# Eight samples' recurrence on the VectorE alone, and the convolution's layer norm freed of a wait for the merge

## The chip, the cores and the metric

The kernel is one program on one core of a Trainium2 chip. Its engines are TensorE (PE, matrix products), VectorE (DVE), ScalarE (ACT), GpSimd (POOL) and SyncE (SP, whose queue issues nearly all DMAs). Each engine takes its instructions in the order in which they stand in its queue and waits at an instruction until the semaphores of that instruction are reached. The metric is the time of one execution on the device in microseconds (us), as the median of several runs.

## The reference, cut to what matters

One layer of a hybrid decoder. 512 tokens of a prompt and one token each of 8 samples (520 columns in all) go through an RWKV-7 branch and a convolution branch side by side; both are projected, weighted by sigmoid gates (the merge) and sent through an output projection, a gate and a last norm. The two places that the change touches are the samples' recurrence step and the convolution's layer norm with its two SiLU gates:

```
def step(S, inp):                              # S: value_dim x key_dim, per sample and head
    r_t, w_t, k_t, v_t, a_t, b_t = inp
    sa = einsum('bhij,bhj->bhi', S, a_t)
    S = S * w_t[:, :, None, :] + sa[..., None] * b_t[:, :, None, :] + v_t[..., None] * k_t[:, :, None, :]
    return S, einsum('bhij,bhj->bhi', S, r_t)
...
cm = mean(cf); cv = mean(square(cf - cm))      # over the 1024 channels
cf = (cf - cm) * rsqrt(cv + LN_EPS) * cln_g + cln_b
cb = silu(cf) * silu(gate_b)
y_b = einsum('btc,cd->btd', cb, w_proj_b)
m = sigmoid(ga) * y_a + sigmoid(gb) * y_b      # ga, gb: the merge projections
h = x + einsum('btd,de->bte', m, w_out)
```

## The kernel before

Activations lie channels on partitions, 520 tokens along the free dimension. All large products run in a split form: each operand is a rounded high part and a low part (hi, lo for activations, wh, wl for weights), and each 128x128 weight block costs three pairs of matmuls of 260 columns, hi by wh, lo by wh, hi by wl (`step`, L211). For each weight tile ACT writes wh (L154) and DVE writes wl (a subtraction, recorded like all helper calls at L67). A `gemm` is 16 such steps (8 in the two projections of the branches), and its sum in PSUM (tile mm) is then taken by DVE.

The program runs in stages: a first accumulation; then for each of eight pairs of heads p the projections of that pair (`gemm`), beside which the prompt's recurrence of the pair (`wkv`) and the depthwise convolution (`conv`, 30 multiply-adds of DVE into tile c for each of 8 channel tiles) run as generators; then the rest of the 32 `merge` projections (DVE scales mm into p, ACT takes the sigmoid, SP stores it); then the projection of the RWKV branch (`gemm(8, ya)`), of the convolution branch (`gemm(8, yb)`), the output product, and the gate with the last norm.

The order of PE's and DVE's queues is written out by the program itself. `tick` is called once after each step and lets every live generator go on by one stretch: `yield n` means wait n steps, `yield ROOM` means go on in a later step, and only if the planned DVE clock is at most LAG = 1.0 us ahead of the planned PE clock. `Paced` charges both clocks; an operation that is issued through `gps` (GpSimd) is charged to the same DVE clock as one issued through `vec`. The weights' subtractions, the scaling of mm and the small operations of the prompt's recurrence are issued without asking for room. ACT, POOL and SP take their instructions in an order that the framework sets from the program.

The change lies in two generators. `sample` (two of them share the eight groups i0 of eight state rows) treats a group of 8 x 64 state entries per partition in nine operations of 128x512: t1 = s0\*a, t2 = v\*k, sa = sum(t1), s0 = s0\*w, t1 = sa\*b, t1 = t1 + t2, s0 = s0 + t1 (then stored by SP), t2 = s0\*r, oso = sum(t2). Four of the nine, t1 = s0\*a, t2 = v\*k, s0 = s0\*w and t2 = s0\*r, go through `gps`. `samples` starts the two, waits for both, and carries their output through PE and a small norm; `rest` runs `samples`, starts `reload` (the eight tiles ya for the first branch projection, each loaded, then split by ACT and DVE) and then runs `lnorm`. `rest` begins when the last pair's recurrence loop begins, with `conv` of the last channel tile not yet at its end.

`lnorm` sums tile csum over channels, subtracts the mean from the eight convolution tiles c, sums their squares, takes the reciprocal of the root (L865), waits until all merges are issued (`flag["merged"]`, L867), and then, for each tile, loads the gate gb (SP), scales c (DVE), applies gain and bias and the sigmoid (ACT), multiplies (DVE, then POOL with the gate), and splits the product into hi and lo (`hlp`) in the pool xp, whose buffers hold the layer's input until the last merge has read it.

The prompt's recurrence is what PE waits for step by step: for each of eight chunks, PE multiplies (aux<-suv,ar), ACT copies (xs, L642), five steps later PE multiplies (aux<-xs,ttb), ACT copies (suv, L648), five steps later PE multiplies (aux<-suv,bn), DVE writes the next suv, five steps later the next chunk begins (for the last pair; `ly`).

Of the kernel before, what the change touches and what calls it, by code (L numbers as in the profile page):

```python
# [12 lines left out]
ALU = mybir.AluOpType  # L13
# [4 lines left out]
P = 128  # L18
# [33 lines left out]
ROOM = -1  # L52
# [18 lines left out]
def body(nc, tc, a):  # L71
    with ExitStack() as es:
# [4 lines left out]
        xp = pool("xp", bufs=2 * KD)  # L77
# [19 lines left out]
        def work(us):  # L97
            clock["dve"] = max(clock["dve"], clock["pe"]) + us
# [4 lines left out]
        vec = Paced(nc.vector, lambda name, n: work(0.0069 * n if name == "reciprocal" else (0.2 if name == "scalar_tensor_tensor" else 0.14) + 0.00107 * n))  # L103
        gps = Paced(nc.gpsimd, lambda name, n: work(0.0014 * n if n > 64 else 0.05))
        pe = Paced(nc.tensor, pe_work)

        def tt(eng, out, x, y, op):
            eng.tensor_tensor(out, x, y, op=op)
# [189 lines left out]
        def colsum(lhsT, hi, lo, n):  # L298

            out = []  # L300
            step = n if n <= 512 else HF
            for h in range(0, n, step):
                o = aux()
                pe.matmul(o[:, :step], lhsT=lhsT, rhs=hi[:, h:h + step], start=True, stop=False)
                pe.matmul(o[:, :step], lhsT=lhsT, rhs=lo[:, h:h + step], start=False, stop=True)
                out.append((h, step, o))
            return out
# [46 lines left out]
        def gt(name):  # L354
            return gp.tile([P, T], F32, name=name, tag="g")

        def parts(x, n=T):
            hi = gp.tile([P, T], F32R, name="hi", tag="g")[:, :n]
            lo = gp.tile([P, T], F32R, name="lo", tag="g")[:, :n]
            act(hi, x, AF.Copy)  # L360
            yield 2
            tt(vec, lo, x, hi.bitcast(F32), ALU.subtract)
            return hi, lo

        def et(name):
            return kp.tile([P, T], F32, name=name, tag="e", bufs=4)
# [48 lines left out]
        flag = {"samples": 0, "out": -1, "inv": -1, "done": -1, "loop": -1, "conv": 0, "yp": None, "merged": False}  # L415
# [345 lines left out]
        def sample(sv, bc8, oso, i0s):  # L761
            nxt = None
            for i0 in i0s:
                s0 = nxt
                for i in ((i0,) if s0 is None else ()) + ((i0 + 16,) if i0 + 16 in i0s else ()):
                    nxt = gp.tile([P, 8, 64], F32, name="s0", tag="g")
                    dma(out=nxt, in_=a["swkv"][:, i:i + 8, :])
                    s0 = s0 or nxt
                t1 = gp.tile([P, 8, 64], F32, name="t1", tag="g")
                t2 = gp.tile([P, 8, 64], F32, name="t2", tag="g")  # L770
                sa = kp.tile([P, 8], F32, name="sa", bufs=2)
                if i0 < 16:
                    yield 8
                tt(gps, t1, s0, bc8(1), ALU.mult)
                yield ROOM
                tt(gps, t2, sv[:, 5, i0:i0 + 8].unsqueeze(2).to_broadcast([P, 8, 64]), bc8(3), ALU.mult)
                yield 3
                yield ROOM
                vec.tensor_reduce(sa, t1, axis=AX.X, op=ALU.add)
                tt(gps, s0, s0, bc8(0), ALU.mult)  # L780
                yield ROOM
                tt(vec, t1, sa.unsqueeze(2).to_broadcast([P, 8, 64]), bc8(2), ALU.mult)
                yield ROOM
                tt(vec, t1, t1, t2, ALU.add)
                yield 1
                yield ROOM
                tt(vec, s0, s0, t1, ALU.add)
                dma(out=a["wkv_s"][:, i0:i0 + 8, :], in_=s0)
                yield 1
                tt(gps, t2, s0, bc8(4), ALU.mult)  # L790
                yield 5
                yield ROOM
                vec.tensor_reduce(oso[:, i0:i0 + 8], t2, axis=AX.X, op=ALU.add)
            flag["samples"] += 1
# [31 lines left out]
        cbs, yb = [], []  # L826


        def lnorm():
            ch, cl = yield from parts(csum)  # L830
            for i in range(4):
                c = gt("c")
                dma(out=c, in_=c_d[i])
                cbs.append(c)
            yield 10
            mean = gt("mean")
            for h, n, o in colsum(oner, ch, cl, T):
                act(mean[:, h:h + n], o[:, :n], AF.Copy, scale=1.0 / 1024)
            yield 3
            vs = None  # L840
            for i in range(8):
                c = cbs[i]
                yield ROOM
                tt(vec, c, c, mean, ALU.subtract)
                sq = et("sq")
                act(sq, c, AF.Square)  # L846
                if i < 4:
                    x = gt("c")
                    dma(out=x, in_=c_d[i + 4])
                    cbs.append(x)  # L850
                yield 3
                if vs is None:
                    vs = sq
                else:
                    yield ROOM
                    tt(vec, vs, vs, sq, ALU.add)
            yield 1
            vh, vl = yield from parts(vs)
            yield 4
            rl = mean  # L860
            for h, n, o in colsum(oner, vh, vl, T):
                act(rl[:, h:h + n], o[:, :n], AF.Sqrt, scale=1.0 / 1024, bias=eps[:, 1:2])
            yield 5
            for h in range(0, T, 130):
                vec.reciprocal(rl[:, h:h + 130], rl[:, h:h + 130])  # L865
                yield ROOM
            while not flag["merged"]:  # L867
                yield 1
            prev = None
            for i in range(9):  # L870
                if i < 8:
                    c = cbs[i]
                    g = et("gb")
                    dma(out=g, in_=gb_d[i])
                    yield ROOM
                    tt(vec, c, c, rl, ALU.mult)
                    act(c, c, AF.Identity, scale=col(O_CG, i), bias=col(O_CBB, i))
                    s = et("sg")
                    act(s, c, AF.Sigmoid)
                    yield 3  # L880
                if prev:
                    c1, g1, s1 = prev
                    yield ROOM
                    tt(vec, c1, c1, s1, ALU.mult)
                    tt(gps, c1, c1, g1, ALU.mult)
                    yield 4
                    yb.append((yield from hlp(xp, c1, "x")))
                prev = (c, g, s)

        ya = []  # L890

# [12 lines left out]
        def rest():  # L904
            yield 12
            yield from samples()
            start(reload(), 2)
            while flag["conv"] < 8:
                yield 1
            yield from lnorm()  # L910
# [43 lines left out]
        def hlp(pl, x, tag):  # L954
            hi = pl.tile([P, T], F32R, name="hi", tag=tag)
            lo = pl.tile([P, T], F32R, name="lo", tag=tag)
            act(hi, x, AF.Copy)
            yield 2
            yield ROOM
            tt(vec, lo, x, hi.bitcast(F32), ALU.subtract)  # L960
            return hi, lo
# [21 lines left out]
        def st(name):  # L983
            return sp2.tile([P, T], F32, name=name, tag="s")
# [11 lines left out]
        for j in range(KD):  # L996
            x = st("x")
# [12 lines left out]
        for k in range(2):  # L1010
            x = st("p")
# [153 lines left out]
```

## Time and profile before

| | us |
|---|---|
| median of 3 runs (1774.98 to 1776.42) | 1775.76 |
| the profiled execution, whole | 1775.46 |
| its span in the trace | 1773.7 |
| PE busy | 1749.6 |
| DVE busy | 1249.7 |
| ACT busy | 831.9 |
| POOL busy | 200.0 |

The span runs from the first to the last instruction in the trace. PE means matmuls, PEld weight loads; busy time of an engine is the time in which it had an instruction at work, waits not counted. In the table of waits each row names an engine and line, what ended its wait, the sum, the count and the longest. In a timeline each row has start, duration, engine, line, operation, the tile written and those read, the shape, a count of merged neighbours, and, in brackets, the engine's idle time just before it and what ended that. Rows of windows give the busy time of every engine in a stretch and the TensorE clock that was granted (1.00 is full speed).

### The profile page before, as it was taken

What the parts mean: (1) busy time and instruction counts of PE and PEld (TensorE: products, weight loads), DVE (VectorE), ACT (ScalarE), POOL (GpSimd) and SP (SyncE); (2) the same over time, 40 slices, a digit from 0 to 9 for tenths busy, and PEclk for the clock granted to TensorE, in tenths of its full rate; (3) what the DMA queues carried; (4) which work ended last, traced back from release to release, by engine and by line L of the source; (5) the groups of instructions that cost most, each with busy time, mean ns of one, the idle gap of its engine ahead of it and who ended that gap; (6) DMA issues with size and microseconds to landing.
All of it is one profiled execution on the core that took longest, in us unless ns stands there. A gap on an engine that the chain in (4) does not pass through costs nothing.

```text
span 1773.7 us, 36966 instructions
## 1 busy us (share of the span) xinstructions
PE 1749.6 (99%) x15064; PEld 1738.9 (98%) x15064; DVE 1249.7 (70%) x2379; ACT 831.9 (47%) x1644; POOL 200.0 (11%) x237
## 2 busy tenths in 40 slices
PE   9999999999999999999999899999999999999996
PEld 9999999999999999999999899999999999999996
DVE  7568889889888889888988977565444333335457
ACT  6734546455455464474554433454333222243344
POOL 1100100001001010010010225001122000011111
PEclk9999999999999999999999999999999999999998
DMA  7252233333333433334324444477655332252233
GB/s 236 81 135 91 87 120 103 97 104 104 116 92 88 121 96 109 103 93 111 103 93 114 126 141 140 132 239 242 198 182 189 110 120 95 86 201 96 89 102 109
DMA packets 122186, 221.35 MB, mean 125 GB/s; under 512 B 48016, under 2 KB 57360, under 8 KB 122016
## 3 DMA queue, kind: packets, MB, share of 16 engines
q1 hardware_dynamic: 120416, 217.39, 39.3%
q8 instruction: 118, 1.93, 0.4%
q10 hardware_dynamic: 1600, 1.60, 0.3%
q14 instruction: 52, 0.43, 0.1%
HBM read 189.61 MB, written 29.34 MB: 123 GB/s over the span
## 4 chain that ended last, share of the span: by engine, by line
PE 95%; DVE 3%; DMA 1%; issue 0%; ACT 0%; POOL 0%; SPq 0%; POOLq 0%; ACTq 0%; DVEq 0%
PE mm L211 87%; PE aux L67 7%; PE aux L211 1%; DVE c L67 1%; DVE wl L67 1%; DMA w<-in_win 1%; DVE h L67 0%; DVE tm L67 0%; DVE ti L67 0%; POOL h L67 0%; DMA s<-in_swkv 0%; DMA x<-in_xT 0%; ACT wh L154 0%; ACT sq L846 0%; DVE sq L67 0%
## 5 line engine op out<-in xcount | busy, mean ns | idle before, releaser
L154 ACT ACTIVATE wh<-w 128x512 fp32r<-128x512 f32 (+1 forms) x541 | 338.8, 628 | 588.1 <-PE mm L211 500.9
L211 PE MATMUL mm<-xh,wh 128*128 128x260 f32 x2784 | 582.9, 291 | 0.2 <-ACT wh L154 0.2
L211 PE MATMUL mm<-xh,wl 128*128 128x260 f32 x2784 | 562.0, 283 | 1.5 <-DVE wl L67 1.5
L211 PE MATMUL mm<-xl,wh 128*128 128x260 f32 x2784 | 561.3, 283 | 0.0
L67 DVE TENSOR_TENSOR wl<-w,wh 128x512 fp32r<-128x512 f32 (+1 forms) x541 | 377.0, 699 | 166.0 <-ACT wh L154 163.4
L211 PEld LDWEIGHTS mm<-xh,wh 128*128 128x128 f32 x2784 | 429.3, 189 | 3.3 <-ACT wh L154 0.7
L211 PEld LDWEIGHTS mm<-xh,wl 128*128 128x128 f32 x2784 | 428.8, 189 | 1.7 <-DVE wl L67 1.7
L211 PEld LDWEIGHTS mm<-xl,wh 128*128 128x128 f32 x2784 | 429.6, 189 | 0.2
L211 PE MATMUL mm<-hi,wl 128*128 128x260 f32 x1600 | 332.9, 283 | 0.2 <-DVE wl L67 0.2
L211 PE MATMUL mm<-lo,wh 128*128 128x260 f32 x1600 | 332.0, 282 | 1.1 <-DVE lo L67 1.1
L211 PE MATMUL mm<-hi,wh 128*128 128x260 f32 x1600 | 332.5, 283 | 0.0
L211 PEld LDWEIGHTS mm<-lo,wh 128*128 128x128 f32 x1600 | 251.1, 188 | 1.4 <-DVE lo L67 1.3
L211 PEld LDWEIGHTS mm<-hi,wh 128*128 128x128 f32 x1600 | 251.5, 189 | 0.0
L211 PEld LDWEIGHTS mm<-hi,wl 128*128 128x128 f32 x1600 | 250.1, 188 | 0.5 <-DVE wl L67 0.5
L67 DVE SCALAR_TENSOR_TENSOR c<-u,prm,c 128x482 f32<-128x482 f32 (+14 forms) x240 | 185.6, 773 | 4.2
L67 DVE TENSOR_TENSOR p<-mm,rs 128x520 f32<-128x520 f32 x78 | 54.2, 695 | 37.1 <-PE mm L211 36.1
L67 DVE TENSOR_REDUCE ti<-tm 128x8 f32<-128x16 f32 (+30 forms) x248 | 73.6, 297 | 8.6
L67 DVE TENSOR_TENSOR tm<-ti,ni 128x16 f32<-128x16 f32 (+30 forms) x248 | 73.7, 297 | 4.9
L67 POOL TENSOR_TENSOR sq<-hi,lo 128x520 f32<-128x520 f32 (+1 forms) x20 | 26.5, 1330 | 353.9 <-DVE one L67 184.0
L67 DVE TENSOR_TENSOR s<-mm,s 128x520 f32<-128x520 f32 x32 | 22.4, 700 | 56.5 <-PE mm L211 53.9
L662 ACT ACTIVATE sf<-suv,epl 64x64 f32<-64x64 f32 x112 | 38.6, 345 | 44.6 <-DVE suv L67 43.0
L67 DVE SCALAR_TENSOR_TENSOR suv<-aux,epl,sf 64x64 f32<-64x64 f32 x96 | 27.2, 283 | 41.4 <-ACT wh L154 20.3
(232 smaller groups left out, 1604.5 us busy)
## 6 DMA issues: line engine op xcount, KB each, us to landing
w<-in_win SPq DMA_DIRECT2D x170, 512.0 KB, 3.8
w<-in_wout SPq DMA_DIRECT2D x32, 512.0 KB, 3.7
w<-in_wpg SPq DMA_DIRECT2D x24, 512.0 KB, 3.6
s<-sga_d SPq DMA_DIRECT2D x32, 260.0 KB, 3.7
w<-in_wpa SPq DMA_DIRECT2D x16, 512.0 KB, 4.1
w<-in_wpb SPq DMA_DIRECT2D x16, 512.0 KB, 3.8
wx<-in_wpg SPq DMA_DIRECT2D x32, 256.0 KB, 3.9
x<-in_xT SPq DMA_DIRECT2D x16, 260.5 KB, 6.4
```

What stands on the lines that cost most here:

```text
L67: return f(*args, **kw)
L154: behind.append(act(wh[:, k], w[:, k], AF.Copy))
L211: nc.tensor.matmul(o[h], lhsT=w[:, used[0] % 4, :], rhs=x[:, h * HF:(h + 1) * HF], start=(k == 0 and i == 0), stop=(k == nk - 1 and i == 2))
L662: act(sf[half(h)], suv[half(h), h, c + 1, :], AF.Copy, scale=epl[half(h), c + 1:c + 2])
```

## The change

In `sample` the four operations that went through `gps` go through `vec`, each asking for room, and the fixed waits of 3, 1, 1 and 5 steps between them are gone. In `lnorm` the wait for `flag["merged"]` stands behind the loop over the tiles, and so does the split into hi and lo, which now runs over the eight tiles one after the other; the wait of 4 steps before each split is gone.

```
@@ sample @@
                 if i0 < 16:
                     yield 8
-                tt(gps, t1, s0, bc8(1), ALU.mult)
-                yield ROOM
-                tt(gps, t2, sv[:, 5, i0:i0 + 8].unsqueeze(2).to_broadcast([P, 8, 64]), bc8(3), ALU.mult)
-                yield 3
+                yield ROOM
+                tt(vec, t1, s0, bc8(1), ALU.mult)
+                yield ROOM
+                tt(vec, t2, sv[:, 5, i0:i0 + 8].unsqueeze(2).to_broadcast([P, 8, 64]), bc8(3), ALU.mult)
                 yield ROOM
                 vec.tensor_reduce(sa, t1, axis=AX.X, op=ALU.add)
-                tt(gps, s0, s0, bc8(0), ALU.mult)
+                yield ROOM
+                tt(vec, s0, s0, bc8(0), ALU.mult)
...
                 dma(out=a["wkv_s"][:, i0:i0 + 8, :], in_=s0)
-                yield 1
-                tt(gps, t2, s0, bc8(4), ALU.mult)
-                yield 5
+                yield ROOM
+                tt(vec, t2, s0, bc8(4), ALU.mult)
                 yield ROOM
@@ lnorm @@
-            while not flag["merged"]:
-                yield 1
             prev = None
             for i in range(9):
...
                     tt(vec, c1, c1, s1, ALU.mult)
                     tt(gps, c1, c1, g1, ALU.mult)
-                    yield 4
-                    yb.append((yield from hlp(xp, c1, "x")))
                 prev = (c, g, s)
+            while not flag["merged"]:
+                yield 1
+            for c in cbs:
+                yb.append((yield from hlp(xp, c, "x")))
```

What this does to the queues, at three places. First DVE's queue where the samples begin, at the end of the last channel tile's convolution (c, csum); suv and oc belong to the prompt's recurrence, t1, t2, s0 and sa to the samples. Before:

```order
L67 TENSOR_TENSOR csum_790<-csum_790,c_12825 128x520
L67 TENSOR_TENSOR wl_13848<-w_13770,wh_13847 128x512
L67 SCALAR_TENSOR_TENSOR suv_13582<-aux_13653,epl_12675,sf_13652 64x64 x2
L67 TENSOR_REDUCE sa_13717<-t1_13715 128x8
L67 TENSOR_TENSOR t1_13715<-sa_13717,sv_13701 128x512
L67 TENSOR_TENSOR wl_13883<-w_13770,wh_13882 128x512
L67 TENSOR_TENSOR t1_13715<-t1_13715,t2_13716 128x512
L67 TENSOR_TENSOR oc_13651<-oc_13651,aux_13653 64x128 x2
```

Now:

```order
L67 TENSOR_TENSOR csum_790<-csum_790,c_12825 128x520
L67 TENSOR_TENSOR t1_13715<-s0_13711,sv_13701 128x512
L67 TENSOR_TENSOR wl_13816<-w_13680,wh_13815 128x512
L67 TENSOR_TENSOR t2_13716<-sv_13701 128x512
L67 TENSOR_REDUCE sa_13717<-t1_13715 128x8
L67 TENSOR_TENSOR s0_13711<-s0_13711,sv_13701 128x512
L67 TENSOR_TENSOR t1_13715<-sa_13717,sv_13701 128x512
L67 TENSOR_TENSOR wl_13849<-w_13770,wh_13848 128x512
L67 SCALAR_TENSOR_TENSOR suv_13582<-aux_13653,epl_12675,sf_13652 64x64 x2
L67 TENSOR_TENSOR t1_13715<-t1_13715,t2_13716 128x512
L67 TENSOR_TENSOR t1_13759<-s0_13755,sv_13701 128x512
L67 TENSOR_TENSOR t2_13760<-sv_13701 128x512
```

The four products of each group stand in DVE's queue behind csum, 32 rows more over the stage; ahead of csum DVE's queue is what it was, but for the convolution's last row (c, 128x511), which now stands ahead of a p and a wl. POOL's queue loses the same 32 rows.

Second, DVE's queue around the last merge (p_15624, p_15647) and the first tile of the RWKV branch's projection (s1_15651<-mm); y is reloaded by `reload`, sq and c are `lnorm`'s. Before:

```order
L67 TENSOR_TENSOR p_15624<-mm_15471,rs_92 128x520
L67 TENSOR_TENSOR c_15453<-c_15453,mean_15405 128x520
L67 TENSOR_TENSOR lo_15621<-y_15564,hi_15620 128x520
L67 TENSOR_TENSOR sq_15451<-sq_15451,sq_15629 128x520
L67 TENSOR_TENSOR c_15492<-c_15492,mean_15405 128x520
L67 TENSOR_TENSOR lo_15636<-y_15618,hi_15635 128x520
L67 TENSOR_TENSOR sq_15451<-sq_15451,sq_15639 128x520
L67 TENSOR_TENSOR c_15540<-c_15540,mean_15405 128x520
L67 TENSOR_TENSOR lo_15647<-y_15633,hi_15646 128x520
L67 TENSOR_TENSOR sq_15451<-sq_15451,sq_15644 128x520
L67 TENSOR_TENSOR wl_15591<-w_15512,wh_15590 128x512
```

Now:

```order
L67 TENSOR_TENSOR lo_15610<-y_15558,hi_15609 128x520
L67 TENSOR_TENSOR sq_15330<-sq_15330,sq_15613 128x520
L67 TENSOR_TENSOR p_15647<-mm_15507,rs_92 128x520
L67 TENSOR_TENSOR wl_15619<-w_15541,wh_15618 128x512
L67 TENSOR_TENSOR c_15464<-c_15464,mean_15284 128x520
L67 TENSOR_TENSOR wl_15656<-w_15541,wh_15655 128x512
L67 TENSOR_TENSOR sq_15330<-sq_15330,sq_15671 128x520
L67 TENSOR_TENSOR s1_15651<-mm_15653,s1_15651 128x520
L67 TENSOR_TENSOR wl_15689<-w_15616,wh_15688 128x512
L67 TENSOR_TENSOR lo_15711<-sq_15330,hi_15710 128x520
```

The samples' end, `reload` and `lnorm` stand one merge projection (16 steps) earlier, so the last split of a y stands ahead of the last p, and the weights' subtractions are spread among the others.

Third, DVE's queue in the RWKV branch's projection, where `lnorm` scales (c by mean, which holds the reciprocal there) and gates (c by sg). Before:

```order
L67 TENSOR_TENSOR s1_16010<-mm_16012,s1_16010 128x520
L67 TENSOR_TENSOR wl_16047<-w_15972,wh_16046 128x512
L67 TENSOR_TENSOR lo_16074<-c_15309,hi_16073 128x520
L67 TENSOR_TENSOR c_15313<-c_15313,mean_15405 128x520
L67 TENSOR_TENSOR wl_16083<-w_15972,wh_16082 128x512
L67 TENSOR_TENSOR c_15311<-c_15311,sg_16006 128x520
L67 TENSOR_TENSOR s1_16078<-mm_16080,s1_16078 128x520
```

Now:

```order
L67 TENSOR_TENSOR s1_16014<-mm_16016,s1_16014 128x520
L67 TENSOR_TENSOR wl_16053<-w_15975,wh_16052 128x512
L67 TENSOR_TENSOR c_15192<-c_15192,sg_16010 128x520
L67 TENSOR_TENSOR c_15371<-c_15371,mean_15284 128x520
L67 TENSOR_TENSOR wl_16090<-w_15975,wh_16089 128x512
L67 TENSOR_TENSOR c_15332<-c_15332,sg_16069 128x520
L67 TENSOR_TENSOR c_15419<-c_15419,mean_15284 128x520
L67 TENSOR_TENSOR s1_16085<-mm_16087,s1_16085 128x520
```

Scaling and gating stand in the RWKV branch's projection before and now, behind the last merge; the splits (lo<-c) move behind the last tile's gate and stand together.

## The prediction

> **What bounds the kernel.** I read the page's busy times first, then PE's own waits, then PE's timeline around them, and only then DVE, POOL and ACT at the same places.
>
> ```profile
> PE 1749.6 (99%) x15064; PEld 1738.9 (98%) x15064; DVE 1249.7 (70%) x2379; ACT 831.9 (47%) x1644; POOL 200.0 (11%) x237
> ...
> 1000.00:1025.00 25.00, 18.86 (x161) 18.08 (x160) 23.72 (x29) 10.01 (x24) 9.15 (x6) 0.86 0.30 103
> ...
> 1175.00:1200.00 25.00, 23.33 (x189) 22.59 (x188) 19.67 (x31) 13.47 (x23) 0.00 (x0) 1.00 0.56 189
> ...
> 1760.00:1773.70 13.70, 0.70 (x2) 0.30 (x2) 7.15 (x7) 0.99 (x2) 5.70 (x4) 0.55 0.51 176
> ```
>
> PE is busy for 99% of the span, so nothing that other engines do matters unless it ends a wait of PE. In stretches of 25 us, PE is full nearly everywhere. Besides the start and the tail of 13.7 us, which this change doesn't touch, it lacks 6.14 us in 1000 to 1025 and 1.67 us in 1175 to 1200. The change works at just these two places: the samples' first products, and the end of the merge. Whatever PE saves there reaches the end of the span undiminished, since PE is full from there to the tail.
>
> PE's timeline names the waits:
>
> ```profile
> 1002.48 0.24 PE L67 MATMUL aux<-tm,yt 32*32 32x32 f32 x2 [0.99 <-ACT yt L601]
> 1002.88 0.69 PE L67 MATMUL aux<-tm,yt 32*32 32x32 f32 x30 [0.16 <-ACT yt L601]
> ...
> 1014.52 0.50 PE L211 MATMUL mm<-xh,wl 128*128 128x260 f32 x2 [1.50 <-DVE wl L67]
> ...
> 1019.25 0.69 PE L67 MATMUL aux<-xs,ttb 128*128 128x64 f32 x2 [3.50 <-ACT xs L642]
> ...
> 1184.33 0.50 PE L211 MATMUL mm<-lo,wh 128*128 128x260 f32 x2 [1.09 <-DVE lo L67]
> ...
> 1185.78 0.51 PE L211 MATMUL mm<-hi,wl 128*128 128x260 f32 x2 [0.25 <-DVE wl L67]
> ...
> 1189.62 0.39 PE L67 MATMUL aux<-lo,cr 128*128 128x260 f32 x1 [0.33 <-DVE lo L67]
> ```
>
> The first four sum to 6.15 us, the last three to 1.67: the two windows are accounted for.
>
> **First gap: POOL slows DVE.** ACT is only the messenger. Its xs stands behind the sigmoid of a p, and that p comes late from DVE:
>
> ```profile
> 1018.08 0.64 ACT L757 ACTIVATE p<-p 128x520 f32<-128x520 f32 x1 [8.42 <-DVE p L67]
> 1018.74 0.45 ACT L642 ACTIVATE xs<-aux 64x64 f32<-64x64 f32 x2
> ```
>
> DVE's queue, and POOL's at the same time:
>
> ```profile
> 995.54 3.53 DVE L67 SCALAR_TENSOR_TENSOR c<-u,prm,c 128x487 f32<-128x487 f32 x2
> 1000.56 1.45 DVE L67 SCALAR_TENSOR_TENSOR c<-u,prm,c 128x489 f32<-128x489 f32 x2
> 1004.33 2.94 DVE L67 SCALAR_TENSOR_TENSOR c<-u,prm,c 128x491 f32<-128x491 f32 x2
> 1007.19 1.77 DVE L67 TENSOR_TENSOR wl<-w,wh 128x512 fp32r<-128x512 f32 x1
> 1008.89 4.97 DVE L67 SCALAR_TENSOR_TENSOR c<-u,prm,c 128x493 f32<-128x493 f32 x4
> 1013.78 0.69 DVE L67 TENSOR_TENSOR wl<-w,wh 128x512 fp32r<-128x512 f32 x1
> 1014.38 3.05 DVE L67 SCALAR_TENSOR_TENSOR c<-u,prm,c 128x497 f32<-128x497 f32 x4
> 1017.36 0.69 DVE L67 TENSOR_TENSOR p<-mm,rs 128x520 f32<-128x520 f32 x1
> ```
>
> ```profile
> 995.58 1.31 POOL L67 TENSOR_TENSOR t<-s,sv 128x512 f32<-128x512 f32 x1 [15.09 <-DMA s<-in_swkv]
> ...
> 1003.82 2.93 POOL L67 TENSOR_TENSOR t<-sv 128x512 f32<-128x512 f32 x2
> ...
> 1010.20 1.60 POOL L67 TENSOR_TENSOR s<-s,sv 128x512 f32<-128x512 f32 x1
> ```
>
> Two multiply-adds of one width take 1.45 us while POOL is idle and 3.53 or 2.94 while it works; four take 3.05 or 4.97; one wl takes 0.69 or 1.77. The excess is 2.08 + 1.49 + 1.08 + 1.92 = 6.57 us, all of it between POOL's first sample product at 995.58 and its last at 1011.80. These POOL rows are what the change removes, and their successors on DVE stand behind csum, past this stretch. So the p at 1017.36 comes at about 1010.8, and xs, which follows within 1.83 us (1018.74 + 0.45 - 1017.36), is ready at 1012.6. PE without its 6.15 us of waiting would ask for it at 1019.25 - 6.15 = 1013.1. The margin is 0.5 us. The wl of 1013.78 would be there at 1007.2, far ahead of PE. The yt wait of 1.15 us lies behind the first excess, 2.08 us, through a p that ACT waits for as well. I take all **6.15 us** as gone; from below, the gain is nothing if POOL isn't the cause.
>
> [...]
>
> After the wait of 3.50 us PE also runs slowly for a while:
>
> ```profile
> 1019.93 5.57 PE mm L211 x30
> ...
> 1029.94 3.65 PE mm L211 x30
> ...
> 1022.00:1024.00 2.00, 2.00 (x11) 2.00 (x11) 1.97 (x4) 0.63 (x1) 0.00 (x0) 0.50 0.66 244
> ```
>
> The same 30 matmuls take 5.57 us where the granted clock is 0.50 and 3.65 at full clock: **1.92 us** that go with the wait. The waits of 1.50 and 1.09 us left the clock at 1.00, so this term hangs on the long one alone.
>
> **Second gap: DVE's burst at the end of the merge.** Before, three splits of y, three sums and four centerings stand between the last p and the first product of the branch's projection, and PE waits for the last split:
>
> ```profile
> 1183.58 0.69 DVE L67 TENSOR_TENSOR lo<-y,hi 128x520 fp32r<-128x520 f32 x1
> ```
>
> Now the last split stands ahead of the last p, and only one centering, one sum and two wl come between p and the product. That moves the split from some 6 us behind the last p to ahead of it, and takes the following wl and lo out of the burst. **1.67 us** go. This comes from the samples' shorter waits (one merge earlier), not from the second edit.
>
> **What the second edit does alone.** In the order now, scaling still begins after the third product of the projection: the reciprocal lies behind the last merge, so the removed wait wasn't binding, and nothing moves into the merge. Only the splits move: the last of them stands three products of the projection earlier, well ahead of the next one, which needs them. The two gate buffers now turn over faster, so SP, at the load of a gate, waits for a product on POOL, and the weights' loads queue behind:
>
> ```profile
> L67 POOL TENSOR_TENSOR c<-c,gb 128x520 f32<-128x520 f32 x8 | 11.5, 1438 | 130.2 <-DVE c L67 124.2 <-ACT c L877 5.9
> ...
> w<-in_wpa SPq DMA_DIRECT2D x16, 512.0 KB, 4.1
> ```
>
> DVE's 0.69 and POOL's 1.44 hold SP for 2.1 us, and 4.1 for the load make 6.2. Three quarter-tiles of weights are converted ahead, each 4 steps of 6 matmuls, 24 x 3.65 / 30 = 2.9 us, so 8.8 us are covered. Cost: 0; without the cover up to 2.1 us for each of six gates.
>
> **The samples on DVE.** 32 operations of 128x512 are added; the sum of their time is of no account, only whether DVE keeps up with PE:
>
> ```profile
> 1024.00:1122.00 98.00, 98.00 (x823) 98.00 (x823) 75.56 (x118) 40.70 (x94) 35.73 (x24) 1.00 0.42 138
> ...
> 1038.55 0.69 DVE L67 TENSOR_REDUCE sa<-t 128x8 f32<-128x512 f32 x1
> 1039.27 0.69 DVE L67 TENSOR_TENSOR t<-sa,sv 128x512 f32<-128x512 f32 x1
> 1039.88 0.68 DVE L67 TENSOR_TENSOR wl<-w,wh 128x512 fp32r<-128x512 f32 x1
> ...
> 1042.67 0.70 DVE L67 TENSOR_TENSOR p<-mm,rs 128x520 f32<-128x520 f32 x1 [0.29 <-PE mm L211]
> ...
> 1055.31 0.70 DVE L67 TENSOR_TENSOR p<-mm,rs 128x520 f32<-128x520 f32 x1 [1.64 <-PE mm L211]
> ```
>
> One merge lasts 12.6 us (p to p), and the new order has 18 rows of DVE in it. A row follows an independent one after 0.61 us and the row that it needs after 0.72: between 11.0 and 13.0 us, and mostly independent, so I take 11.3. At worst DVE falls behind by 0.4 us a merge, 2.8 over seven. What PE waits for is the recurrence's suv:
>
> ```profile
> 1049.17 0.55 PE L67 MATMUL aux<-suv,bn 128*128 128x64 f32 x4
> 1053.22 0.55 PE L67 MATMUL aux<-suv,ar 128*128 128x64 f32 x4
> ...
> 1049.83 0.60 DVE L67 SCALAR_TENSOR_TENSOR suv<-aux,epl,sf 64x64 f32<-64x64 f32 x2 [0.91 <-PE aux L67]
> ```
>
> It is done at 1050.43 and needed at 1053.22: 2.8 us of slack, which even the upper bound just uses up. Cost: 0. [...]
>
> **Sum.** 6.15 + 1.92 + 1.67 = 9.74 us from the profiled 1775.46 (span 1773.7, 1.76 around it): 1765.7. The profiled run lies 0.30 below the median shown, so **1766.0**.
>
> **Rivals.** (1) Less comes back. If DVE regains only half, 3.3 us, xs is ready at 1015.9, PE still waits 2.8 us there, and the gain is 3.35 + 1.67, with the clock's 1.92 or without: 1769 to 1771. For it: a margin of 0.5 us only, and DVE was late already before POOL began. Against: each DVE row is back at its short time as soon as POOL stops.
>
> (2) POOL isn't the cause, and the long rows stay. Then the first gap stays and only 1.67 us go; with one long row a merge (1.08 more) DVE's 11.3 become 12.4 of 12.6 us, so nothing more is lost: 1775.46 - 1.67 + 0.30 = 1774.1. Against it: all the long rows lie in POOL's stretch and none beside it.
>
> (3) Slower: a state load late on DVE. A group's first product waits for its state from memory; POOL could sit there for 15.09 us (row of 995.58) with nobody behind it, but on DVE wl, p and suv stand behind.
>
> ```profile
> s<-in_swkv SPq DMA_DIRECT2D x8, 256.0 KB, 5.1
> ```
>
> Four groups are loaded ahead; the other four loads stand about one merge, 12.6 us, ahead of their use and take 5.1. If SP holds such a load longer than 12.6 - 5.1 + 2.8 = 10.3 us, PE begins to wait. If each of the four were to arrive a load's length, 5.1 us, after DVE asks, it would cost 5.1 - 2.8 + 1.92 of clock, 4.2 each, 17 in all: 1766 + 17 = 1783. Against it: a merge's length is more than twice the load's.
>
> **Chances and range.** Forecast 0.68, (1) 0.14, (2) 0.10, (3) 0.08. What a measurement of this kernel can tell from no change is about 0.2%, 3.6 us, so (1) counts as faster: faster 0.82, same 0.10, slower 0.08. The range takes in the forecast and (1), with 0.8 us of spread between runs: 1764.8 to 1771.5.
>
> **What would show it.** Right: no PE wait over 0.5 us between 995 and 1025, clock 1.00 there, c rows of 0.75 us throughout; PE full in the window of the merge's end; DVE near 9 tenths in the samples' stage with PE full. Wrong: a wait for xs that remains (1); c rows of 1.7 us without POOL (2); DVE rows of t waiting for in_swkv and PE waits for suv (3). If PE waits for wl in the branch's projection behind loads of gb, the second edit costs something.

## The result and the profile after

| | before | after |
|---|---|---|
| median, us (lowest to highest) | 1775.97 (1774.98 to 1776.42) | 1765.02 (1764.70 to 1765.73) |
| profiled execution, us | 1775.46 | 1765.73 |
| its span, us | 1773.7 | 1763.5 |

The ratio after to before is 0.9940, with a 95% interval of 0.9927 to 0.9952: faster by 10.95 us of the medians. The forecast was 1766.0, 0.98 us too high and inside its range.

The page of the changed kernel, busy times of the engines, and its table of what PE waited for (sum, count and longest, us):

```profile
PE 1746.3 (99%) x15064; PEld 1736.0 (98%) x15064; DVE 1256.1 (71%) x2411; ACT 831.7 (47%) x1644; POOL 154.6 (9%) x205
```

```profile
PE aux L1059 <- DVE sq L67: 2.1, 1, 2.1
PE aux L254 <- DVE zero L67: 1.2, 1, 1.2
PE mm L211 <- ACT xh L266: 0.4, 1, 0.4
PE mm L211 <- DVE xl L67: 0.3, 1, 0.3
PE mm L211 <- ACT wh L154: 0.2, 1, 0.2
PE aux L67 <- ACT yt L601: 0.2, 1, 0.2
```

Nothing is left but the start, the tail and 0.16 us for yt: no wl, no xs, no lo. The stretches by window show the same (length; then busy PE, PEld, DVE, ACT, POOL; the granted clock; share and rate of DMA):

```profile
1000.00:1025.00 25.00, 24.82 (x234) 24.45 (x233) 24.41 (x38) 12.95 (x32) 0.00 (x0) 1.00 0.44 145
1024.00:1110.00 86.00, 86.00 (x724) 86.00 (x723) 74.61 (x133) 34.62 (x83) 0.00 (x0) 1.00 0.45 143
...
1175.00:1200.00 25.00, 25.00 (x210) 25.00 (x209) 16.30 (x25) 14.72 (x22) 2.96 (x2) 1.00 0.78 252
```

The first row held 18.86 us of PE at a mean clock of 0.86 before, and holds 24.82 at 1.00 now. In the samples' stage (second row) DVE is busy 74.61 of 86 us, 87%, and PE is full.

DVE's timeline over the first gap (start, duration, engine, line, operation, tile written and tiles read, shape, count):

```profile
996.27 1.49 DVE L67 SCALAR_TENSOR_TENSOR c<-u,prm,c 128x487 f32<-128x487 f32 x2
...
1002.61 1.49 DVE L67 SCALAR_TENSOR_TENSOR c<-u,prm,c 128x491 f32<-128x491 f32 x2
...
1004.61 3.04 DVE L67 SCALAR_TENSOR_TENSOR c<-u,prm,c 128x493 f32<-128x493 f32 x4
...
1011.14 0.69 DVE L67 TENSOR_TENSOR p<-mm,rs 128x520 f32<-128x520 f32 x1
```

Two c take 1.49 us where they took 3.53 and 2.94, four take 3.04 for 4.97, and p comes at 1011.14 instead of 1017.36. What follows from that p, on ACT and on PE:

```profile
1012.53 0.45 ACT L642 ACTIVATE xs<-aux 64x64 f32<-64x64 f32 x2
```

```profile
1013.43 0.33 PE L67 MATMUL aux<-xs,ttb 128*128 128x64 f32 x2
```

xs is ready at 1012.98 and asked for at 1013.43. The margin is 0.45 us.

To see where the gain arose, the same matmul is taken in both traces. First before, then after; the four places lie ahead of the first gap, behind it, and on the two sides of the second:

```profile
947.13 0.33 PE L67 MATMUL aux<-xs,ttb 128*128 128x64 f32 x2
...
1061.09 0.55 PE L67 MATMUL aux<-suv,bn 128*128 128x64 f32 x4
...
1177.61 0.41 PE L211 MATMUL mm<-hi,wh 128*128 128x260 f32 x2
...
1189.96 0.28 PE L67 MATMUL aux<-lo,cr 128*128 128x260 f32 x1
```

```profile
947.67 0.33 PE L67 MATMUL aux<-xs,ttb 128*128 128x64 f32 x2
...
1053.00 0.55 PE L67 MATMUL aux<-suv,bn 128*128 128x64 f32 x4
...
1169.52 0.41 PE L211 MATMUL mm<-hi,wh 128*128 128x260 f32 x2
...
1179.25 0.28 PE L67 MATMUL aux<-lo,cr 128*128 128x260 f32 x1
```

Before minus after is -0.54, then 8.09, 8.09 and 10.71 us. So the changed kernel enters 0.54 us late (its start took longer in this execution), gains **8.63 us** at the first gap, nothing in the samples' stage, and **2.62 us** at the second. Of these 11.25 us the profiled pair of executions shows 9.73: the start takes 0.54, the tail 0.51 (the spans differ by 10.2), and the time outside the span 0.47 (2.23 against 1.76).

### The profile page after: what moved, and what is told of

It reads as the page before. It is cut to its first block, busy times and chain, and to the rows that moved or that the text cites. A ratio compares the mean times of both kernels' runs of the same rounds, so it can differ in the third digit from the quotient of the medians.

```text
span 1763.5 us, 36946 instructions
## 1 busy us (share of the span) xinstructions
PE 1746.3 (99%) x15064; PEld 1736.0 (98%) x15064; DVE 1256.1 (71%) x2411; ACT 831.7 (47%) x1644; POOL 154.6 (9%) x205
## 4 chain that ended last, share of the span: by engine, by line
PE 97%; DVE 1%; DMA 1%; ACT 0%; POOL 0%; issue 0%; SPq 0%; POOLq 0%; DVEq 0%; ACTq 0%
PE mm L211 89%; PE aux L67 7%; PE aux L211 1%; DMA w<-in_win 0%; DVE h L67 0%; DMA x<-in_xT 0%; POOL h L67 0%; DVE wl L67 0%; DVE c L67 0%; DVE rf L67 0%; PE aux L1059 0%; POOLq L1161 0%; SPq L143 0%; ACT wh L154 0%; ACT ttb L615 0%
## 5 line engine op out<-in xcount | busy, mean ns | idle before, releaser
L67 DVE SCALAR_TENSOR_TENSOR c<-u,prm,c 128x482 f32<-128x482 f32 (+14 forms) x240 | 180.2, 751 | 4.3
```

Of the source, the lines that this page charges most:

```text
L67: return f(*args, **kw)
```

## The experiments

Theory: POOL's products slow DVE's two-input rows and so make the first gap, with the fall of the clock behind it; the shorter waits alone close the second gap; the second edit does nothing.

**The two edits apart.** The first kernel has the change in `sample` only; the second has the change in `lnorm` only.

> Only the first edit: the samples' products on DVE with the new waits; the layer norm as before. Theory (POOL's products slow DVE; the samples' earlier end empties the burst at the end of the merge; the second edit does nothing): as the changed kernel, 1765.0 us, 0.5 either way, no PE wait over 0.3 us at either place. Rival (the second edit closes the gap at the end of the merge): 1765.0 + 2.6 = 1767.6, with the waits for lo and wl of the second gap still there.

> Only the second edit: the layer norm's scaling and gating without the wait for the merge, the splits behind; the samples as before. Theory: no change, 1776.0, both gaps as before (6.15 and 1.67 us of PE's waits). Rival (the second edit closes the second gap): 1776.0 - 2.6 = 1773.4.

The first took 1764.60 us (1764.28 to 1765.23; ratio 0.9936, 0.9924 to 0.9949), the second 1775.78 (1774.30 to 1776.75; ratio 0.9999, 0.9991 to 1.0008). The first edit gives all of it. In the second kernel PE's waits are nearly those of before (wl 2.1 us in all for 1.7, yt 0.2 for 1.1):

```profile
PE aux L67 <- ACT xs L642: 3.5, 1, 3.5
PE mm L211 <- DVE wl L67: 2.1, 2, 1.9
...
PE mm L211 <- DVE lo L67: 1.1, 1, 1.1
```

**The first edit in two.** It moves the products to DVE and shortens the waits between them. One kernel has the engine alone (fixed waits as before), one the waits alone (products on POOL); `lnorm` is that of before in both.

```
# engine alone (the four products alike)
- tt(gps, t1, s0, bc8(1), ALU.mult)
+ tt(vec, t1, s0, bc8(1), ALU.mult)
# waits alone
+ yield ROOM
  tt(gps, t1, s0, bc8(1), ALU.mult)
  yield ROOM
  tt(gps, t2, ...)
- yield 3
  yield ROOM
  vec.tensor_reduce(sa, t1, ...)
+ yield ROOM
  tt(gps, s0, s0, bc8(0), ALU.mult)
...
- yield 1
+ yield ROOM
  tt(gps, t2, s0, bc8(4), ALU.mult)
- yield 5
  yield ROOM
```

> Of the first edit only the engine: the four products on DVE, but with the fixed waits of 3, 1, 1 and 5 steps as before; the layer norm as before. Theory: the first gap closes (8.6 us by PE's landmarks), the burst at the merge's end stays, since DVE's order there is that of before: 1776.0 - 8.6 = 1767.4. Rival (the waits and the place in the queue matter, not the engine): PE still waits near the end of the last convolution, 1773 or more.

> Of the first edit only the waits: the products stay on POOL, but the fixed waits are replaced by asking for room; the layer norm as before. Theory: POOL still works beside the last convolution, so the first gap stays; the samples end earlier, so most of the second gap closes: 1776.0 - 2 = 1774. Rival (the waits do it all): 1765 to 1768.

The engine alone: 1767.59 us (1766.74 to 1767.79; ratio 0.9953, 0.9938 to 0.9968). PE has no wait between 990 and 1030, and the second gap is untouched:

```profile
1175.54 0.51 PE L211 MATMUL mm<-lo,wh 128*128 128x260 f32 x2 [1.09 <-DVE lo L67]
...
1177.00 0.51 PE L211 MATMUL mm<-hi,wl 128*128 128x260 f32 x2 [0.25 <-DVE wl L67]
...
1180.83 0.39 PE L67 MATMUL aux<-lo,cr 128*128 128x260 f32 x1 [0.33 <-DVE lo L67]
```

These are the three waits of before to the hundredth. The waits alone: 1772.61 us (1772.03 to 1773.83; ratio 0.9981, 0.9972 to 0.9990), and the other way round: PE is full from 1168 to 1195, and the first gap stays:

```profile
1168.00:1195.00 27.00, 27.00 (x227) 27.00 (x227) 21.20 (x34) 14.24 (x26) 0.00 (x0) 1.00 0.70 239
```

```profile
1018.99 0.69 PE L67 MATMUL aux<-xs,ttb 128*128 128x64 f32 x2 [4.45 <-ACT xs L642]
```

So each half of the edit closes one gap, and the halves nearly add up: 1775.9 - 1767.59 = 8.3 and 1775.9 - 1772.61 = 3.3, together 11.6 beside the 11.3 of both. At the four places used above, the profile of the engine alone gains 9.06 us at the first gap and nothing at the second, that of the waits alone 0.99 and 2.61. I had expected 1774 for the waits alone, a gain too small by a good microsecond. About half of that is the second gap, which I had priced at 2 us. The rest fits the 0.99 at the first gap, where PE no longer waits for wl; whether the shorter waits do that in every execution was not tried, since the second edit alone shows 0.90 there in its profile and gains nothing in its median.

**POOL kept, but later.** Products on POOL with the old waits; the samples start, and load their state, only behind the last convolution tile (`while flag["conv"] < 8: yield 1` at the head of `sample`); `lnorm` as before.

> Kernel before, the products on POOL, but the two sample generators begin (and load their states) only when the last convolution tile is done. Theory: no POOL work beside the last convolution, so c rows stay at 0.75 us and the first gap closes by 8.6 us; the later samples lengthen the burst at the merge's end, which costs 1 to 5 us more than before: 1769 to 1772. Rival (it must be DVE that does the products): the first gap stays, 1776 or more.

1772.09 us (1771.59 to 1774.12; ratio 0.9978, 0.9969 to 0.9988). With POOL quiet until 1025.80 the first gap is gone and p comes at 1010.78, though the products are still POOL's. Most of what was won there is lost at the merge's end, where the late samples lengthen DVE's burst:

```profile
1174.36 0.50 PE L211 MATMUL mm<-hi,wh 128*128 128x260 f32 x2 [1.26 <-ACT hi L959]
1176.85 0.50 PE L211 MATMUL mm<-lo,wh 128*128 128x260 f32 x2 [1.98 <-DVE lo L67]
...
1178.92 0.80 PE L211 MATMUL mm<-lo,wh 128*128 128x260 f32 x2 [1.10 <-DVE lo L67]
```

From place to place, the merge's end takes 5.83 us longer than before, above the 1 to 5 expected, and the granted clock falls there too: 0.65, 0.50, 0.50 and 0.65 in the 2 us windows from 1178 to 1186.

**POOL's work put back into the changed kernel.** Products that nobody reads, at the head of the first two groups (eight) or of the first alone (four), and, as a third kernel, work of the same length in which POOL only writes.

```
+ if i0 < 16:                       # four products: if i0 == 0
+     for i in (1, 0, 4, 3):
+         nc.gpsimd.tensor_tensor(scr, s0, bc8(i), op=ALU.mult)
```

```
+ if i0 < 16:
+     nc.gpsimd.tensor_copy(scr[:, 0, 0:8], s0[:, 0, 0:8])
+     for _ in range(7):
+         nc.gpsimd.memset(big, 0.0)
```

> Changed kernel, with eight products of the samples' states put on POOL beside the last convolution, into a tile that nobody reads (about 12 us of POOL, two inputs in SBUF). Nothing of the needed work moves. Theory: DVE's rows there double again, xs is some 5 us late, and the long wait brings the clock down: 1765.0 + 6 to 8.6 = 1771 to 1773.6. Rival (the gap came from DVE's or ACT's order, not from POOL): 1765.0.

> As the run with eight, but four products on POOL (about 6 us). Theory: DVE loses some 3.3 us, the margin at xs takes 0.5 of it, PE waits 2 to 3 us in all; if the clock only falls after a wait of over 3 us, 1767 to 1768.2; if it falls after any wait of 2 us, 1769 to 1770. Rival (POOL plays no part): 1765.0.

> As the run with eight products, but POOL only writes: one small copy and seven fills of 128x1024, twice, about the same time of POOL at the same place. [...] If any POOL work at that place slows DVE: 1771 to 1773.6.

Eight products: 1772.95 us (1772.53 to 1774.50; ratio 0.9984, 0.9975 to 0.9994). Four: 1769.17 (1767.19 to 1770.16; ratio 0.9960, 0.9945 to 0.9975). Writes alone: 1764.78 (1764.21 to 1766.50; ratio 0.9938, 0.9924 to 0.9953), the time of the changed kernel and not the 1771 to 1773.6 expected if any POOL work slows DVE. With eight products the gap is back, DVE first, then POOL:

```profile
1000.42 3.05 DVE L67 SCALAR_TENSOR_TENSOR c<-u,prm,c 128x489 f32<-128x489 f32 x2
...
1006.81 3.43 DVE L67 SCALAR_TENSOR_TENSOR c<-u,prm,c 128x491 f32<-128x491 f32 x2
...
1017.28 0.69 DVE L67 TENSOR_TENSOR p<-mm,rs 128x520 f32<-128x520 f32 x1
```

```profile
996.15 13.56 POOL L776 TENSOR_TENSOR ni<-s,sv 128x512 f32<-128x512 f32 x8 [15.09 <-DVE on L67]
```

With 14 fills of about the same total length DVE is as fast as with POOL idle:

```profile
996.25 7.03 POOL L777 MEMSET ni<- 128x1024 f32 x7
...
1003.95 7.04 POOL L777 MEMSET ni<- 128x1024 f32 x7
```

```profile
1001.75 1.49 DVE L67 SCALAR_TENSOR_TENSOR c<-u,prm,c 128x491 f32<-128x491 f32 x2
```

DVE does not pay for POOL's being busy: 14.07 us of POOL writes cost the kernel nothing (1764.78), and 13.56 us of products, which read two tiles in SBUF, cost 7.9 (1772.95 - 1765.02). In these kernels it is POOL's reading, as far as products set against fills can show it. In the kernel with eight products, only DVE's rows with two inputs in SBUF are slowed: in the 13.56 us of POOL's reads, two c take 2.39, 3.05 and 3.43 us and a wl 1.16 and 1.78 (1.45 to 1.49 and 0.68 to 0.69 in the changed kernel), while rows that take one input from PSUM keep their time (p<-mm,rs 0.69 us at 998.36, bv<-aux 0.74 at 1005.09), and so does the one with a single input (tm<-ti 0.43 at 1000.05). Nor is DVE blocked for all of POOL's work: from the c at 996.05 to the p at 1017.28 it takes 21.23 us, where the changed kernel takes 14.87 (996.27 to 1011.14), so it loses 6.4 us beside 13.56 of reads.

**Does a short wait lower the clock, too?** The four products gave a spread of 3 us between executions, and their profile a clock of 0.50 behind one wait of 2.05 us, for which the prediction had no rule: it had seen 1.00 behind waits of 1.50 and 1.09 and 0.50 behind one of 3.50. Two more profiles of this kernel:

> The kernel with four unneeded POOL products once more, for a second profile. In its first one, a single PE wait of 2.05 us for xs was followed by a granted clock of 0.50 for some 4 us, and the execution took 1770.16 us; the others took 1767.19 to 1769.57. Theory A, such a wait lowers the clock in some executions and not in others, by when it falls: this profile shows the same wait (1.8 to 2.3 us), and either 1.00 throughout with a span near 1766, or again 0.50 with a span near 1768. Rival, a wait of this length always lowers the clock and the spread has another origin: 0.50 for about 4 us here too, whatever the time.

> The same kernel, a third profile. Theory A: at least one of the two new profiles shows the wait without the fall of the clock, and that one's span is shorter by 1.5 to 2 us. Rival: all three show it.

They took 1767.91 and 1769.06 us. PE's wait and the windows that hold the fall, from the first profile, the second and the third:

```profile
1016.51 0.43 PE L67 MATMUL aux<-xs,ttb 128*128 128x64 f32 x2 [2.05 <-ACT xs L642]
...
1016.00:1018.00 2.00, 1.49 (x9) 1.49 (x10) 1.96 (x4) 1.51 (x5) 0.00 (x0) 0.80 0.35 133
1018.00:1020.00 2.00, 2.00 (x11) 2.00 (x10) 1.93 (x3) 0.63 (x1) 0.00 (x0) 0.50 0.50 117
1020.00:1022.00 2.00, 2.00 (x16) 2.00 (x16) 1.42 (x3) 0.00 (x0) 0.00 (x0) 0.85 0.39 145
```

```profile
1003.09 0.24 PE L67 MATMUL aux<-tm,yt 32*32 32x32 f32 x2 [1.25 <-ACT yt L601]
...
1004.00:1006.00 2.00, 2.00 (x21) 1.96 (x16) 1.97 (x4) 1.28 (x3) 0.00 (x0) 0.73 0.42 123
1006.00:1008.00 2.00, 2.00 (x12) 2.00 (x11) 1.97 (x4) 0.65 (x2) 0.00 (x0) 0.50 0.70 270
1008.00:1010.00 2.00, 2.00 (x17) 2.00 (x17) 1.89 (x4) 1.39 (x4) 0.00 (x0) 0.91 0.04 8
```

```profile
1015.73 0.43 PE L67 MATMUL aux<-xs,ttb 128*128 128x64 f32 x2 [2.03 <-ACT xs L642]
...
1016.00:1018.00 2.00, 2.00 (x14) 2.00 (x14) 1.97 (x4) 0.81 (x4) 0.00 (x0) 0.68 0.35 133
1018.00:1020.00 2.00, 2.00 (x11) 2.00 (x10) 1.97 (x4) 0.58 (x1) 0.00 (x0) 0.50 0.85 233
1020.00:1022.00 2.00, 2.00 (x19) 2.00 (x18) 0.80 (x2) 0.00 (x0) 0.00 (x0) 0.96 0.07 29
```

My theory that such a wait lowers the clock only now and then falls: all three profiles show the fall. Its other part, that the wait is the same each time, falls too. The same four products delay other rows of DVE from one execution to the next (the first two c take 2.39 us and the next two 3.06 in the first profile, 3.49 and 2.15 in the second), so PE waits 1.25 us for yt in one and 2.05 us for xs in another. Over the stretch from the xs matmul near 948 to the suv matmul near 1057, the three profiles take 109.33, 108.12 and 108.94 us, so this makes 1.21 of the 2.25 us between the first and the second; what makes the rest of the spread was not looked for.

**The tail.** The last four output tiles of the changed kernel are scaled on POOL in 5.70 us, beside four operations of DVE in 5.22. Here DVE scales all tiles (`ON_POOL = ()`, with the groups of output transfers to match).

> The changed kernel with the merge's last four tiles of the tail (4 POOL products of 5.70 us in all at 1753 us, beside DVE's 4 of 5.22 us, in the profile of the changed kernel) moved to DVE too, and the last groups of output transfers issued in a matching order on the two queues. Theory A, the two engines' products slow each other in the tail as they did in the first gap: DVE alone does the eight in about 8 x 0.75 = 6 us or less, the last product isn't later than before and the end comes up to 1 us earlier, 1764.0 us. Rival, the tail is bound by its output transfers or by the products' sum: no change, 1765.0, or up to 1.5 us later (1766.5) if DVE alone takes longer than the two did side by side.

1764.44 us (1763.62 to 1765.18; ratio 0.9936, 0.9923 to 0.9950) against 1765.02 for the changed kernel: between the two expectations, the ranges overlap, and nothing is decided. The scaling gets shorter, 4.76 us in five operations of DVE, but the span ends 10.15 us behind the reciprocal (1752.15 to 1762.3) where it was 10.45 (1753.05 to 1763.5), so 0.3 us come through in this pair of profiles.

## Why the prediction was right, and where its sizes were off

**What bounds the kernel**: right. PE's idle time was the quantity to count, and nothing that was won at the gaps was given back: the four places differ by 8.09 and still 8.09 us across the samples' stage.

**First gap, POOL slows DVE**: right, and shown from both sides. Without POOL's reads the rows are short (the changed kernel, POOL later, writes only); with them put back the gap returns. That the margin at xs would be 0.5 us was right as well: 0.45. The rival that only half comes back is so refuted for this change, though by a margin that four products use up. The excess of DVE's rows was a little over the 6.57 us counted: one row was left out, bv<-bv,sl, which took 1.10 us before (at 1003.31) and takes 0.69 now. That POOL isn't the cause is refuted by the writes-only run against the eight products.

**The clock**: right that it returns to 1.00, wrong in the size and the rule. The prediction priced it by 30 matmuls, 1.92 us. By the 2 us windows of before, 0.82, 0.50, 0.50, 0.50 and 0.97 between 1016 and 1026, and with the clock at either 1.00 or 0.50, as windows of 0.25 us show it there (1.00 up to 1017.25, 0.50 from 1017.50 to 1024.00, 1.00 from 1024.25), it was down for 0.72 + 6 + 0.12 = 6.84 us, from 1017.28 to 1024.12. So it began in the wait and lasted over the two xs matmuls ahead of those 30, too (0.69 us for the 0.33 of now). The same matmuls, from xs on, before and after:

```profile
1024.15 0.40 PE L211 MATMUL mm<-xl,wh 128*128 128x260 f32 x2
```

```profile
1016.05 0.41 PE L211 MATMUL mm<-xl,wh 128*128 128x260 f32 x2
```

From the xs matmul to this one it is 4.90 us before (from 1019.25) and 2.62 now (from 1013.43), so the clock cost **2.28 us**. With 6.15 - 0.16 of waits that makes 8.27 of the 8.63; the rest is of the kind shown under the second gap, a wait that costs more than its idle time (the one of 1.50 us here cost 1.76). The sentence that the term "hangs on the long one alone" doesn't hold as a rule: in the runs with four products, waits of 2.05 and 1.25 us were enough.

**Second gap**: right in its cause (the waits alone close it, the engine alone doesn't, the second edit doesn't), mis-sized: 1.67 predicted, **2.62** measured. The step that failed took idle time for the whole cost of a wait. Before, PE's rows at this place read:

```profile
1182.59 0.40 PE L211 MATMUL mm<-hi,wl 128*128 128x260 f32 x2
1182.83 0.40 PE L211 MATMUL mm<-hi,wh 128*128 128x260 f32 x2
...
1184.67 0.40 PE L211 MATMUL mm<-hi,wl 128*128 128x260 f32 x2
```

Pairs follow one another every 0.24 us. The pair that waited began at 1184.33, 1.50 behind its forerunner, and the next came 0.34 later: 1.84 instead of 0.48, so a wait with 1.09 us of idle cost 1.36. The pair ahead of the wait counts as busy for its whole 0.40 us, not for the 0.24 to the next, and the one behind it for 0.50; that is about 0.27 us for each of the three waits (0.52 for the one of 0.25, 0.60 for the one of 0.33), 0.8 of the missing 0.95. The rest lies where no idle time is recorded: the pair at 1182.25 began 0.31 behind its forerunner, and the next 0.34 later, 0.17 us more than at 0.24 each.

**The second edit**: right, nothing (0.9999).

**The samples on DVE**: right. DVE keeps up: PE doesn't wait for it in this stage, and DVE waits in each chunk of the recurrence, in most of them for PE.

```profile
1065.57 0.60 DVE L67 SCALAR_TENSOR_TENSOR suv<-aux,epl,sf 64x64 f32<-64x64 f32 x2 [1.18 <-PE aux L67]
```

About 1.2 us of 12 are free in this chunk, as the estimate of 11.3 in 12.6 had it. suv is done at 1066.17 and PE takes it at 1068.96, the slack of 2.8 us from before. No row of t waits for its state from memory, so the slower rival did not happen.

**The sum**: the two terms that were too small by 0.56 and 0.95 are the whole difference at the gaps, 11.25 for 9.74. That the profiled pair shows 9.73 is chance: start, tail and the time outside the span took 1.52 in it.

## What to carry to other kernels

Before work is moved to POOL to relieve DVE, see whether it reads SBUF beside DVE's two-input rows: eight products on an otherwise idle engine cost 8 us by making the busy one late, and 14 us of fills cost nothing. Price a wait of PE at its idle time plus what the pairs beside it lose (0.27 us here), and read the granted clock in windows of 2 us behind it, also where the wait is short (the clock was at 0.50 behind one of 1.25 us). Where two halves of an edit act at different places, run each alone; here either half looks like an answer to the whole.

## What was not expected of the hardware

The clock fell for 3.4 us or for twice that, and the wait does not tell which. Worked out as above from the 2 us windows, the low stretch is 3.40 us in the first profile with four products (0.80, 0.50, 0.85), 3.44 in the second (0.73, 0.50, 0.91) and in the third (0.68, 0.50, 0.96), and 6.84 before the change. One and the same wait of 3.50 us for xs goes with 6.84 before and with 3.40 in the kernel with eight products (0.71, 0.50, 0.94 from 1018 to 1024). Nor does its length tell when the fall comes, or whether. It came 2.7 us after the wait of 2.05 us began in the first profile with four products (1014.46, the fall at 1017.2), 3.0 us after the one of 2.03 began in the third, 3.2 us after the one of 3.50 began with eight products, but 1.5 us after the one of 3.50 began in the kernel before, where a wait of 1.50 us had ended at 1014.52. A wait of 1.43 us with eight products (until 1010.90) was passed over, the clock staying at 1.00 up to 1018, while 1.41 us in the second profile with four, with 0.93 us of 32x32 matmuls between and behind, had the fall at 1004.9. What decides between these cases, and what sets the two lengths, was not tried by itself.
